# Two transformer blocks in one kernel: the convolution's weights on VectorE, a nested block inverse, more weight buffers and another order of transposes

## The chip, the cores and the metric

The kernel runs on one core of a Trainium2 chip, as one launch. Times are microseconds of device time, from the first to the last instruction of an execution and what the launch adds around it. Before the change the median of three runs is 3477.03 us (3469.45 to 3480.14). The engines are TensorE (PE in the trace; PEld is its weight load), VectorE (DVE), ScalarE (ACT), GpSimd (POOL) and SyncE (SP), which here issues nearly all DMAs. Each engine works through its own list of instructions in a fixed order and waits for the others at semaphores.

## The reference, cut to what matters

The model has 512 tokens of width 1024, a context of 256 tokens, and float32 throughout. Block 1 has two layers, block 2 two more:

```python
def first_block(x, c, ...):
    for i in range(2):
        shift, scale, gate = split(silu(c) @ mix_ada_w[i] + mix_ada_b[i], 3)
        h = x * (1 + scale) + shift
        y = _sgu_pool_mixer(h, ...) if i == 0 else _conformer_conv(h, ...)
        x = layer_norm(ALPHA * x + (1 + gate) * y)
        ...                                  # the same with ffn_ada_w and _conv_ffn
def _conformer_conv(h, w_in, dw, dw_b, ln_g, ln_b, w_out):
    a, g = split(h @ w_in, 2)                # 1024 channels each
    z = a * sigmoid(g)
    z = depthwise_conv(z, dw) + dw_b         # 31 taps a channel
    return silu(layer_norm(z)) @ w_out
def second_block(x, c, ctx, c_ctx, ...):
    for i in range(2):
        ml, mc = silu(c) @ w_ada[i] + b_ada[i], silu(c_ctx) @ w_ada[i] + b_ada[i]   # 6 chunks each
        u_lat, u_ctx = modulate(h_lat, ...), modulate(h_ctx, ...)   # rms_norm(h) * (1 + scale) + shift
        o = even_mixer(...) if i == 0 else odd_mixer(...)
        ...                                  # gated residuals and sqrelu_mlp, for context too in layer 0
def rwkv7_scan(f, d, s0, reverse):           # in even_mixer, forward and backward, 8 heads of 64
    def step(state, inp):
        sa = einsum(state, -kk_t)
        state = state * w_t + sa * (kk_t * a_t) + v_t * k_t
        return state, einsum(state, r_t)
```

## The kernel before, in words

**Matmuls.** Float32 matmuls are done as three matmuls of rounded parts: each operand is split in a high part (a rounding cast) and a low part (the difference), and `mm3` (L300) multiplies hi*hi, hi*lo and lo*hi. Weights come by `weights` (L280): SP loads a raw tile of 128x1024, for output weights the raw tile is multiplied by a gate (L287), ScalarE casts the high part (L289), and the low part is a difference (L290) on VectorE, or on the engine that `eng` names. The names in the trace end in the use: `wlo_cvin` is the low part of the convolution's input weights, `wraw_dn` a raw tile of output weights, `hTlo` the low part of transposed tokens.

**Order.** The code is written once through, and a scheduler puts the instructions of each engine in a list at build time; tile pools with a fixed number of buffers make an allocation wait for the last reader. Modulation (the products with `*_ada_w`) is cut into pieces that stand in the list `todo`; `fill` (L269) runs the next one wherever the code calls it, so that these matmuls (`adaps`, L209) lie between others. A piece of 512 columns has 4 weight loads of 512 KB on SP, 16 matmuls with 32 output rows each, a copy `adarows` on ScalarE and a store on SP. The first modulation (`ada_first`, L249) is done at the start, 4 pieces with whole 1 MB tiles from three buffers.

**The convolution** (`mixer1`, L584). For each of 8 channel blocks `gated` projects two times 128 channels (tile `cvps`, weights `cvin` with low parts on GpSimd) and multiplies by a sigmoid. Five blocks and 19 taps of a sixth are convolved on VectorE, one instruction a tap over 512 tokens (L621, L619; 169 of them in all); two blocks and 12 taps are convolved on TensorE with diagonal weights (`conv_pe`, tile `cvacc`): VectorE clears the borders, splits the block into `zh` and `zl` (L278 at the call L635) when `conv_pe` comes to it, one block later than its gate. Then the result is transposed (`cvt`), its statistics are taken on VectorE (L675), a square root follows by Newton steps, the result is normalised, transposed back and multiplied by `w_out`, whose first half of weights is prepared on GpSimd and whose second half on VectorE.

**The recurrence** (`recurrence`, L1346, with `operators`, L1447). The scan over 768 positions runs as six steps of 128 positions in two directions, each with 8 heads, so 12 blocks. A block needs the inverse of a unit lower triangular matrix of 64 per head and half. Its diagonal blocks of 16 are inverted on VectorE; GpSimd expands these to full tiles `X` and its transpose `XT`, and masks the matrix M for level 16 and level 32 (`MM`). Then per level: U = MM*XT (8 matmuls `pV`, copied by ScalarE), and `X` or `XT` gets X*U added (`pX`, addition L1483 on VectorE). Then `pW` multiplies by the operand `Aw`, and `pD` follows.

**The second block** starts by transposing its tokens and its context into `hT` (`hT2`, L861, with a parameter `first` that puts the context ahead), tile `hTps`, after their norms.

## Time and profile before

| what | us |
|---|---|
| median of three runs | 3477.03 |
| the profiled execution's own time | 3472.81 |
| its span, first to last instruction | 3471.0 |
| TensorE busy | 3216.5 (93%) |
| VectorE busy | 2053.2 (59%) |
| ScalarE busy | 1305.7 (38%) |
| GpSimd busy | 397.2 (11%) |

The trace is of one execution. Its stages, from the start of the span: first mixer to 192 us, feed-forward to 633, the convolution to about 914, feed-forward to 1338, the second block's first mixer with its projections to 1629, windowed attention to 1752, the recurrence to about 2110, feed-forward to 2727, the odd mixer to 3106, feed-forward to the end. A timeline row is: start, duration, engine, line, operation, output <- inputs, shape, how many instructions it stands for, and in brackets the idle time before it with what ended it. A group row ends with busy time, mean ns of one, and the idle time before the group by releaser. Line numbers are those of the kernel before.

### The profile page before, as it was taken

The numbers are of one execution on the slowest core, as the hardware profiler recorded it, in microseconds if no ns is written. First come the engines' busy times: TensorE is split into PE (matmuls) and PEld (weight loads), VectorE is DVE, ScalarE is ACT, GpSimd is POOL, SyncE is SP. The second block draws the span as 40 slices with busy tenths as digits, with TensorE's granted clock in tenths as the row PEclk, the third lists the DMA queues.
The fourth block names the chain that finished last, engine by engine and source line by source line (L and its number), as shares of the span: only waits on it lengthen the run. The fifth ranks groups of instructions, "written<-read, shape, count | busy, mean of one in ns | idle before, by whom it ended". The sixth has DMA issues, their size and how long they took to land. (4 is left out here: it accounts for less than half of the span.)

```text
span 3471.0 us, 50354 instructions
## 1 busy us (share of the span) xinstructions
PE 3216.5 (93%) x20031; PEld 2612.9 (75%) x20031; DVE 2053.2 (59%) x3772; ACT 1305.7 (38%) x2150; POOL 397.2 (11%) x218
## 2 busy tenths in 40 slices
PE   8989999868999998987898799999999998999998
PEld 5677777746776776875688798788888787878887
DVE  4675554897755567586767667533333735763445
ACT  3243332317423334443543334422222525753222
POOL 0020000540200000023033331010000200010001
PEclk9999999989999998998989899999999999999999
DMA  7645565440266432445322215672222365143332
GB/s 253 202 134 178 175 212 177 133 161 25 86 195 206 125 105 96 124 122 164 90 67 66 64 53 171 142 152 79 65 63 67 122 155 216 63 138 104 97 97 85
DMA packets 520693, 436.67 MB, mean 126 GB/s; under 512 B 91924, under 2 KB 450042, under 8 KB 518922
## 3 DMA queue, kind: packets, MB, share of 16 engines
q1 hardware_dynamic: 520458, 433.45, 41.4%
q8 instruction: 158, 2.59, 0.3%
q14 instruction: 77, 0.63, 0.1%
HBM read 368.96 MB, written 63.78 MB: 125 GB/s over the span
## 5 line engine op out<-in xcount | busy, mean ns | idle before, releaser
L302 PE MATMUL dnps<-whi_dn,hidh 128*128 128x512 f32 x1120 | 442.0, 395 | 3.5 <-ACT hidh L277 2.0
L303 PE MATMUL dnps<-wlo_dn,hidh 128*128 128x512 f32 x1120 | 438.9, 392 | 0.3
L304 PE MATMUL dnps<-whi_dn,hidl 128*128 128x512 f32 x1120 | 435.4, 391 | 1.2 <-DVE hidl L278 1.2
L290 DVE TENSOR_TENSOR wlo_dn<-wraw_dn,whi_dn 128x1024 fp32r<-128x1024 f32 x136 | 167.2, 1230 | 239.1 <-ACT whi_dn L289 238.3
L302 PE MATMUL upps<-hThi,whi_up 128*128 128x512 f32 (+1 forms) x768 | 295.7, 387 | 6.8 <-DVE hThi L277 6.7
L303 PE MATMUL upps<-hTlo,whi_up 128*128 128x512 f32 (+1 forms) x768 | 293.0, 383 | 4.8 <-DVE hTlo L278 4.8
L304 PE MATMUL upps<-hThi,wlo_up 128*128 128x512 f32 (+1 forms) x768 | 290.3, 379 | 0.0
L424 DVE TENSOR_TENSOR acc<-dnps,acc 128x512 f32<-128x512 f32 x200 | 136.7, 687 | 201.7 <-PE dnps L304 201.2
L302 PEld LDWEIGHTS dnps<-whi_dn,hidh 128*128 128x128 f32 x1120 | 210.2, 188 | 60.9 <-ACT hidh L277 7.0
L289 ACT CAST whi_dn<-wraw_dn 128x1024 fp32r<-128x1024 f32 x140 | 147.1, 1051 | 273.7 <-PE dnps L304 101.5
L303 PEld LDWEIGHTS dnps<-wlo_dn,hidh 128*128 128x128 f32 x1120 | 210.5, 188 | 47.1 <-issue 2.7
L304 PEld LDWEIGHTS dnps<-whi_dn,hidl 128*128 128x128 f32 x1120 | 209.8, 188 | 46.7 <-DVE hidl L278 3.4
L303 PE MATMUL up2ps<-hTlo,whi_ff 128*128 128x512 f32 (+1 forms) x576 | 214.5, 373 | 3.4 <-DVE hTlo L278 3.0
L302 PE MATMUL up2ps<-hThi,whi_ff 128*128 128x512 f32 (+1 forms) x576 | 212.7, 371 | 2.4 <-DVE hThi L277 2.4
L304 PE MATMUL up2ps<-hThi,wlo_ff 128*128 128x512 f32 (+1 forms) x576 | 212.1, 369 | 0.0
L290 DVE TENSOR_TENSOR wlo_up<-wraw_up,whi_up 128x1024 fp32r<-128x1024 f32 x88 | 111.1, 1262 | 135.5 <-ACT whi_up L289 134.6
L302 PEld LDWEIGHTS upps<-hThi,whi_up 128*128 128x128 f32 x768 | 147.2, 192 | 54.1 <-issue 12.4
L824 POOL TENSOR_TENSOR ag<-acc,gg 128x1024 f32<-128x1024 f32 x20 | 49.2, 2458 | 1124.8 <-DVE acc L424 1093.5
L303 PEld LDWEIGHTS upps<-hTlo,whi_up 128*128 128x128 f32 x768 | 147.5, 192 | 39.1 <-issue 9.9
L304 PEld LDWEIGHTS upps<-hThi,wlo_up 128*128 128x128 f32 x768 | 147.8, 193 | 26.1 <-issue 0.8
L289 ACT CAST whi_ff<-wraw_ff 128x1024 fp32r<-128x1024 f32 x64 | 67.2, 1052 | 245.9 <-PE dnps L304 202.3
L290 DVE TENSOR_TENSOR wlo_ff<-wraw_ff,whi_ff 128x1024 fp32r<-128x1024 f32 x64 | 80.8, 1264 | 126.7 <-ACT whi_ff L289 126.4
(528 smaller groups left out, 7431.0 us busy)
## 6 DMA issues: line engine op xcount, KB each, us to landing
adaw<-in_w_ada_dram SPq DMA_DIRECT2D x96, 512.0 KB
wraw_up<-in_ffn_w_up_dram SPq DMA_DIRECT2D x88, 512.0 KB
wraw_ff<-in_w_ff_dram SPq DMA_DIRECT2D x64, 512.0 KB
wraw_dn<-in_w_ff_dram SPq DMA_DIRECT2D x64, 512.0 KB
adaw<-in_ffn_ada_w_dram SPq DMA_DIRECT2D x48, 512.0 KB
wraw_dn<-in_ffn_w_down_dram SPq DMA_DIRECT2D x44, 512.0 KB
adaw<-in_mix_ada_w_dram SPq DMA_DIRECT2D x32, 512.0 KB
ab<-ab SPq DMA_DIRECT2D x32, 384.0 KB
```

The costliest lines, as they stand in the source:

```text
L289: nc.scalar.copy(hi, raw)
L290: (eng or nc.vector).tensor_tensor(lo, raw, hi, SUB)
L302: mm(out, a[0], b[0], start=first, stop=False)
L303: mm(out, a[0], b[1], start=False, stop=False)
L304: mm(out, a[1], b[0], start=False, stop=last)
L424: nc.vector.tensor_tensor(acc[:, t, c], p, acc[:, t, c], ADD)
L824: nc.gpsimd.tensor_tensor(ag, a, gg[:, 0 if t < NT else 1, :], MUL)
```

## The change

1. One mask `lo` (below the diagonal blocks of 16) takes the place of the masks for levels 16 and 32.
2. Modulation pieces have 256 columns where they had 512, so twice as many pieces and stores with half the size each; both raw tiles of a piece are loaded ahead of its matmuls. `fill` is called at more places: ahead of each weight in `ffn1`, in `mixer0` and in `gated`.
3. `ada_first` has 16 more tiles of 128x512 (four more 1 MB buffers), taken from the hidden tiles, so that all but the last of its loads have a buffer of their own.
4. In `mixer1` the low parts of the `cvin` weights and the gate products and low parts of the first half of `w_out` go from GpSimd to VectorE. `rounded` makes `zh`, `zl` and the rounded taps right behind the gate of a block that TensorE convolves; `conv_pe` gets them ready.
5. `operators`: the inverse by two levels becomes a nested form. NT is one product of MM and X (8 matmuls `pV`); then the operand is multiplied three times by NT, each time with the first operand added. Direction 0 multiplies by the diagonal inverse first (`pW`), direction 1 last, so direction 0 needs one expansion and direction 1 two.
6. `hT2` is called with `first=True`: the context is transposed ahead of the tokens.

Cut to its core (the list `todo` is cut anew to the same work in twice as many pieces, and the buffers of the recurrence are renamed):

```diff
+    c4.put("lo", np.concatenate([(t // 16 > u // 16) & (p[:, None] // 64 == q) for q in range(2)], 1))
...
     def ada_part(self, w, sil, c0, bufs=None):
 
-        nc = self.nc
-        acc = self.ps.tile([128, 512], F32, tag="tr", name="adaps", bufs=2)
+
+        nc = self.nc
         n = 512 if bufs else 256
-        for c in range(0, 512, n):
-            for h in range(0, KD, 4):
-                raw = bufs.pop(0) if bufs else self.adap.tile([128, 4, 256], F32, tag="adaw", name="adaw", bufs=self.nadaw)
-                nc.sync.dma_start(raw, w[128 * h:128 * h + 512, c0 + c:c0 + c + n].rearrange("(k p) c -> p k c", p=128))
+        acc = self.ps.tile([128, n], F32, tag="tr", name="adaps", bufs=2)
+        raw = []
+        for h in range(0, KD, 4):
+            b = bufs.pop(0) if bufs else self.adap.tile([128, 4, 256], F32, tag="adaw", name="adaw", bufs=self.nadaw)
+            if isinstance(b, list):
                 for k in range(4):
-                    nc.tensor.matmul(acc[32 * k:32 * k + 32, c:c + n], sil[:, h + k, :], raw[:, k, :], start=h == 0, stop=h > 0)
-        rows = self.wp.tile([128, 512], F32, tag="adar", name="adarows", bufs=1)
+                    nc.sync.dma_start(b[k], w[128 * (h + k):128 * (h + k) + 128, c0:c0 + n])
+            else:
+                nc.sync.dma_start(b, w[128 * h:128 * h + 512, c0:c0 + n].rearrange("(k p) c -> p k c", p=128))
+                b = [b[:, k] for k in range(4)]
+            raw.append(b)
+        for h, r in zip(range(0, KD, 4), raw):
+            for k in range(4):
+                nc.tensor.matmul(acc[32 * k:32 * k + 32], sil[:, h + k, :], r[k], start=h == 0, stop=h > 0)
+        rows = self.wp.tile([128, n], F32, tag="adar", name="adarows", bufs=1)
         nc.scalar.copy(rows, acc)
         return rows
 
     def ada_store(self, w, sil, c0, dst):
 
-        rows = self.ada_part(w, sil, c0)
-        for m in range(dst.shape[0]):
-            self.nc.sync.dma_start(dst[m, :, c0:c0 + 512], rows[m::32, :])
+        def piece(c):
+            rows = self.ada_part(w, sil, c)
+            for m in range(dst.shape[0]):
+                self.nc.sync.dma_start(dst[m, :, c:c + 256], rows[m::32, :])
+        return [partial(piece, c) for c in (c0, c0 + 256)]
...
-        bufs = [big[:, j] for j in range(3)]
+        hid = [b.bitcast(F32) for i in range(8) for b in self.hid(i)]
+        bufs = [big[:, j] for j in range(3)] + [hid[4 * j:4 * j + 4] for j in range(4)] + [big[:, 0]]
...
         def gated(f):
-            self.fill()
             pp = []
             for ff in (f, f + KD):
-                w = self.w_up(w_in, 128 * ff, "cvin", nc.gpsimd)
+                self.fill()
+                w = self.w_up(w_in, 128 * ff, "cvin")
...
-        def conv_pe(f):
+        def rounded(f):
...
+            return zh, zl, wh, wl
+
+        def conv_pe(f, zh, zl, wh, wl):
...
+        parts = []
         for j, f in enumerate(order):
             gated(f)
+            if f in taps_pe:
+                parts.append((f, *rounded(f)))
             for _ in range(14 if j else 0):
                 next(taps)
             if j >= 6:
-                conv_pe(order[j - 1])
+                conv_pe(*parts.pop(0))
                 for _ in range(12 if j == 6 else 24):
                     next(taps, None)
...
-            self.down(w_out, src[:4], acc, True, gate=gate, x=x, eng=nc.gpsimd)
+            self.down(w_out, src[:4], acc, True, gate=gate, x=x)
...
-            X, XT = (v8(bufs[x][d]) for x in ("X", "XT"))
-            for x, t in ((1, XT), (0, X)):
+            X, XT, Y = v8(bufs["X"]), v8(bufs["XT"][d]), v8(bufs["Y"][d])
+            for x, t in ((1, XT), (0, X))[:1 + d]:
...
-            for b in (16, 32):
-                U = v8(R.tile([128, 1024], F32, tag=f"tD{d}", name="U", bufs=2))
+            NT = v8(R.tile([128, 1024], F32, tag=f"tD{d}", name="NT", bufs=2))
+            for hs in H4:
+                nc.scalar.copy(NT[:, hs], mm4("pV", *((XT, MM) if d else (MM, XT)), hs))
+            if not d:
                 for hs in H4:
-                    nc.scalar.copy(U[:, hs], mm4("pV", MM[b], XT, hs))
-                for tr in ((1, 0) if b == 16 else (1 - d,)):
-                    for hs in H4:
-                        t = (XT if tr else X)[:, hs]
-                        vec.tensor_tensor(t, mm4("pX", *((X, U) if tr else (U, X)), hs), t, ADD)
-            XT = X if d == 1 else XT
-            for hs in H4:
-                nc.scalar.copy(Aw[:, hs], mm4("pW", XT, Aw, hs))
+                    nc.scalar.copy(Y[:, hs], mm4("pW", XT, Aw, hs))
+            first, at, to = (Aw, Aw, Y) if d else (Y, Y, Aw)
+            for _ in range(3):
+                for hs in H4:
+                    vec.tensor_tensor(to[:, hs], mm4("pX", NT, at, hs), first[:, hs], ADD)
+                at = to
+            if d:
+                for hs in H4:
+                    nc.scalar.copy(Aw[:, hs], mm4("pW", X, at, hs))
...
-                hT = self.hT2(n, mods)
+                hT = self.hT2(n, mods, first=True)
```

The lists of the engines show the change at these places. VectorE at the split for channel block 7 in the convolution, before: `hidl` with different numbers are the gated channel blocks, `hidh` their convolved results, L621 is a tap.

```order
L621 SCALAR_TENSOR_TENSOR hidh_5057<-hidl_5058,vec_e,hidh_5057 128x507
L621 SCALAR_TENSOR_TENSOR hidh_5055<-hidl_5056,vec_e,hidh_5055 128x506
L621 SCALAR_TENSOR_TENSOR hidh_5057<-hidl_5058,vec_e,hidh_5057 128x506
L621 SCALAR_TENSOR_TENSOR hidh_5055<-hidl_5056,vec_e,hidh_5055 128x505
L631 MEMSET zh 128x15
L632 MEMSET zh 128x15
L631 MEMSET zl 128x15
L632 MEMSET zl 128x15
L603 TENSOR_TENSOR hidl_5064<-cvps,sg 128x512
L278 TENSOR_TENSOR zl<-hidl_5066,zh 128x512
```

Now, at the same split (L285 is the split, L610 the gate product, L628 a tap):

```order
L639 MEMSET zh 128x15
L638 MEMSET zl 128x15
L639 MEMSET zl 128x15
L628 SCALAR_TENSOR_TENSOR hidh_5195<-hidl_5196,vec_e,hidh_5195 128x503
L610 TENSOR_TENSOR hidl_5204<-cvps,sg 128x512
L628 SCALAR_TENSOR_TENSOR hidh_5193<-hidl_5194,vec_e,hidh_5193 128x504
L628 SCALAR_TENSOR_TENSOR hidh_5195<-hidl_5196,vec_e,hidh_5195 128x504
L628 SCALAR_TENSOR_TENSOR hidh_5193<-hidl_5194,vec_e,hidh_5193 128x505
L285 TENSOR_TENSOR zl<-hidl_5204,zh 128x512
L628 SCALAR_TENSOR_TENSOR hidh_5195<-hidl_5196,vec_e,hidh_5195 128x505
L628 SCALAR_TENSOR_TENSOR hidh_5193<-hidl_5194,vec_e,hidh_5193 128x506
L628 SCALAR_TENSOR_TENSOR hidh_5195<-hidl_5196,vec_e,hidh_5195 128x506
```

The split `zl` of a block stood one block's taps behind that block's gate product; it now stands three taps behind it.

VectorE at the end of the convolution, where the statistics (`cvst`) are followed by the square root's steps (`newt`), before:

```order
L621 SCALAR_TENSOR_TENSOR hidh_5059<-hidl_5060,vec_e,hidh_5059 128x498
L675 BN_STATS cvst<-cvt 128x6
L621 SCALAR_TENSOR_TENSOR hidh_5059<-hidl_5060,vec_e,hidh_5059 128x497
L675 BN_STATS cvst<-cvt 128x6 x14
L687 BN_AGGR cvmv<-cvst 128x2 x4
L689 COPY cvvar<-cvmv 128x4
L353 TENSOR_SCALAR newt<-cvvar 128x4
L354 TENSOR_SCALAR newt<-newt 128x4
L361 TENSOR_TENSOR newt<-newt 128x4
L362 TENSOR_TENSOR newt<-newt 128x4
L363 SCALAR_TENSOR_TENSOR newt<-newt 128x4
```

And now:

```order
L688 BN_STATS cvst<-cvt 128x6 x2
L297 TENSOR_TENSOR wlo_dn<-wraw_dn,whi_dn 128x1024
L688 BN_STATS cvst<-cvt 128x6 x4
L700 BN_AGGR cvmv<-cvst 128x2 x4
L294 TENSOR_TENSOR wraw_dn<-wraw_dn,gate 128x1024
L702 COPY cvvar<-cvmv 128x4
L360 TENSOR_SCALAR newt<-cvvar 128x4
L361 TENSOR_SCALAR newt<-newt 128x4
L294 TENSOR_TENSOR wraw_dn<-wraw_dn,gate 128x1024
L368 TENSOR_TENSOR newt<-newt 128x4
L297 TENSOR_TENSOR wlo_dn<-wraw_dn,whi_dn 128x1024
L369 TENSOR_TENSOR newt<-newt 128x4
```

Output weights (L294, L297) that stood ahead of the last taps now lie behind the statistics and between the steps; the statistics themselves lie between the last taps.

TensorE in the recurrence, one block of direction 1, before:

```order
L323 MATMUL pD<-big 128x128 x16
L323 MATMUL pV<-big 128x128 x8
L323 MATMUL pX<-U,big 128x128 x8
L323 MATMUL pX<-big,U 128x128 x8
L323 MATMUL pV<-big 128x128 x8
L323 MATMUL pX<-big,U 128x128 x8
L323 MATMUL pW<-big 128x128 x8
L323 MATMUL pD<-big 128x128 x16
L323 MATMUL pz<-Z,big 64x64 x16
```

And now:

```order
L330 MATMUL pD<-big 128x128 x16
L330 MATMUL pV<-big 128x128 x8
L330 MATMUL pX<-big,NT 128x128 x24
L330 MATMUL pW<-big 128x128 x8
L330 MATMUL pD<-big 128x128 x16
L330 MATMUL pz<-Z,big 64x64 x16
L330 MATMUL PM<-AB 64x64 x15
```

One group of eight `pV` is gone, and the three rounds of `pX` stand in one run of 24, each round reading what the round before it left.

## Rows read from the trace of the kernel before

**Rows 1.** The page, part 1: busy time of each engine, its share, instructions.

```profile
PE 3216.5 (93%) x20031; PEld 2612.9 (75%) x20031; DVE 2053.2 (59%) x3772; ACT 1305.7 (38%) x2150; POOL 397.2 (11%) x218
```

**Rows 2.** Table by stage: us, busy PE PEld DVE ACT POOL, clock, DMA.

```profile
700.00:760.00 60.00, 49.66 (x279) 33.62 (x278) 60.00 (x64) 11.78 (x15) 34.53 (x10) 0.94 0.53 169
...
1752.00:2100.00 348.00, 309.76 (x3830) 288.01 (x3827) 243.20 (x515) 124.11 (x226) 124.05 (x80) 0.90 0.24 68
```

**Rows 3.** Timeline of PE, convolution: start, us, line, idle before and releaser.

```profile
745.21 1.08 PE L209 MATMUL adaps<-adaw,sil 128*32 128x256 f32 x8 [5.77 <-DMA adaw<-in_w_ada_dram]
...
776.83 0.76 PE L302 MATMUL cvacc<-zh,dg 128*128 128x512 f32 x1 [19.04 <-DVE zl L632]
...
802.90 0.47 PE L302 MATMUL cvacc<-zh,dg 128*128 128x512 f32 x1 [3.71 <-DVE zl L632]
```

**Rows 4.** Timeline of DVE, convolution.

```profile
735.35 24.65 DVE L621 SCALAR_TENSOR_TENSOR hidh<-hidl,vec_e,hidh 128x498 f32<-128x498 f32 x19
...
760.53 16.11 DVE L621 SCALAR_TENSOR_TENSOR hidh<-hidl,vec_e,hidh 128x509 f32<-128x509 f32 x18
...
777.24 0.68 DVE L278 TENSOR_TENSOR zl<-hidl,zh 128x512 fp32r<-128x512 f32 x1
...
813.61 21.80 DVE L621 SCALAR_TENSOR_TENSOR hidh<-hidl,vec_e,hidh 128x497 f32<-128x497 f32 x28
848.77 0.43 DVE L675 BATCH_NORM_STATS2 cvst<-cvt 128x6 f32<-128x256 f32 x1 [13.36 <-PE cvt L667]
```

**Rows 5.** Groups of POOL, 633 to 855 us: busy, mean ns, idle before.

```profile
L290 POOL TENSOR_TENSOR wlo_cvin<-wraw_cvin,whi_cvin 128x1024 fp32r<-128x1024 f32 x15 | 39.7, 2654 | 40.0 <-ACT whi_cvin L289 36.9 <-PE adaps L209 3.1
L287 POOL TENSOR_TENSOR wraw_dn<-wraw_dn,gate 128x1024 f32<-128x1024 f32 x4 | 16.8, 4207 | 17.5 <-DMA wraw_dn<-in_cv_w_out_dram 8.4 <-PE adaps L209 5.1 <-issue 4.0
L290 POOL TENSOR_TENSOR wlo_dn<-wraw_dn,whi_dn 128x1024 fp32r<-128x1024 f32 x4 | 10.8, 2696 | 25.9 <-ACT whi_dn L289 25.9
```

**Rows 6.** Groups of DVE, 633 to 855 us: busy, mean ns, idle.

```profile
L621 DVE SCALAR_TENSOR_TENSOR hidh<-hidl,vec_e,hidh 128x503 f32<-128x503 f32 (+15 forms) x169 | 147.2, 916 | 1.9
L278 DVE TENSOR_TENSOR hTlo<-hTf,hThi 128x256 fp32r<-128x256 f32 x16 | 14.8, 939 | 0.2
```

**Rows 7.** Groups of DVE, 813 to 836 us, GpSimd idle.

```profile
L621 DVE SCALAR_TENSOR_TENSOR hidh<-hidl,vec_e,hidh 128x499 f32<-128x499 f32 (+15 forms) x29 | 21.6, 745 | 1.0
```

**Rows 8.** Groups of DVE, first feed-forward stage, 192 to 633 us.

```profile
L290 DVE TENSOR_TENSOR wlo_up<-wraw_up,whi_up 128x1024 fp32r<-128x1024 f32 x41 | 50.2, 1224 | 67.8 <-ACT whi_up L289 67.4
...
L278 DVE TENSOR_TENSOR hTlo<-hTf,hThi 128x256 fp32r<-128x256 f32 x16 | 10.6, 680 | 0.1
```

**Rows 9.** Waits of SP, 640 to 800 us: total, times, longest.

```profile
SPq L285 <- POOL wlo_dn L290: 29.1, 4, 8.5
SPq L218 <- ACT adarows L211: 9.3, 6, 2.1
```

**Rows 10.** Timeline of PE in one block of the recurrence.

```profile
1870.32 1.95 PE L323 MATMUL pV<-big 128*128 128x128 f32 x16
1872.11 2.00 PE L323 MATMUL pX<-big,U 128*128 128x128 f32 x16
1873.99 2.05 PE L323 MATMUL pW<-big 128*128 128x128 f32 x16
```

**Rows 11.** Groups of POOL in the recurrence, 1752 to 2100 us.

```profile
L1460 POOL TENSOR_TENSOR big<-Xd,consts 128x1024 f32<-128x1024 f32 x12 | 29.2, 2437 | 22.4 <-PE pV L323 15.9 <-PE pW L323 6.4
```

**Rows 12.** Groups of PE in the recurrence: the state products.

```profile
L323 PE MATMUL P<-AB 64*64 64x64 f32 x1152 | 48.5, 235 | 18.4 <-DVE big L1422 15.0 <-DVE WhThi L1422 2.9 <-ACT M L1383 0.2
```

**Rows 13.** Timeline of DVE in the same block of the recurrence.

```profile
1873.24 0.69 DVE L1483 TENSOR_TENSOR big<-pX,big 128x512 f32<-128x512 f32 x1 [2.04 <-PE pX L323]
```

**Rows 14.** Timeline of PE at the second block's start.

```profile
1345.99 0.69 PE L337 MATMUL hTps<-consts,acc 128*128 128x128 f32 x2 [7.75 <-ACT acc L814]
```

**Rows 15.** Table of windows at the start, columns as in rows 2.

```profile
25.00:30.00 5.00, 5.00 (x18) 3.95 (x17) 4.14 (x12) 2.87 (x6) 0.00 (x0) 0.56 1.05 409
```

**Rows 16.** Timeline of PE at the start.

```profile
30.34 1.07 PE L209 MATMUL adaps<-adaw,silc 128*32 128x512 f32 x8
```

More of the change, by code (lines that the diff above doesn't have):

```diff
@@ L521, in mixer0 @@
         for h in range(4):
-            if h == 2:
-                self.fill()
+            self.fill()
             w = self.w_up(w_in, 128 * h, "inu")
@@ L543, in mixer0 @@
         for g, win in enumerate(WINDOWS):
+            self.fill()
             w = self.w_up(w_in, 1024 + 128 * g, "inz")
@@ L752, in ada @@
             i, part = phases[k]
-            return [lambda q=q: self.ada_store(ap[f"{part}_ada_w"][i], sil, 512 * q, ada1[k]) for q in qs]
-        ada2 = [lambda j=j: self.ada_store(ap["w_ada_2"][j // 12], sil2, 512 * (j % 12), self.ada_d[j // 12])
-                for j in range(24)]
+            return [f for q in qs for f in self.ada_store(ap[f"{part}_ada_w"][i], sil, 512 * q, ada1[k])]
+        ada2 = [f for j in range(24) for f in self.ada_store(ap["w_ada_2"][j // 12], sil2, 512 * (j % 12), self.ada_d[j // 12])]
         def columns():
```

27 lines of the change are left out of this document (10 added, 17 removed).

## Prediction

> **What bounds the kernel now.** I read the page's busy shares, then the table by stage, then the timelines of the stages with idle on TensorE. TensorE is busy 3216.5 of 3471.0 us [rows 1]: over the whole span it is the bound, and only its idle time, or matmuls that go, can be won. Two of the stages that the change touches have much of that idle. One is the second mixer of the first block (the convolution, 633 to 860 us). In its middle VectorE is busy 60.00 of 60 us and TensorE 49.66 [rows 2], and TensorE stops 5.77, 19.04 and 3.71 us in single waits [rows 3]. The other is the recurrence (1752 to 2100), where TensorE is busy 309.76 of 348 us [rows 2]: there the matmuls themselves are the bound.
>
> Why VectorE is the bound of the convolution is seen in its taps. With GpSimd beside it, 19 of them take 24.65 us, 1.30 each; later, with GpSimd idle, 28 take 21.80, 0.78 each [rows 4]. The long wait of 19.04 ends with `zl`, a split of one channel block, which VectorE issues at 777.24 behind a run of 18 taps that began at 760.53: its order is fixed, so TensorE waits for taps that it does not need. After the last tap (813.61 + 21.80 = 835.4) VectorE itself is idle 13.36 us, until TensorE, late by those waits, has transposed the result [rows 4].
>
> **The change part by part.** All sums are made against the profiled run, 3472.8 us; it lies 4.2 us under the median of the three runs.
>
> *Convolution: work moved from GpSimd to VectorE.* GpSimd loses 15 differences of 2.65 us, 4 products with the gate of 4.21 and 4 differences of 2.70: 39.7 + 16.8 + 10.8 = 67.3 us [rows 5]. What that beside it cost VectorE: 169 taps at 0.916 against 0.745 when alone, 28.9 us; 16 differences `hTlo` at 0.939 against 0.680 in the feed-forward stage, 4.1 [rows 6, 7, 8]. Together 33.0 us go. What VectorE gains in work: 15 + 8 operations of 128x1024 at 1.224 [rows 8] are 28.2 us. So its load falls by only 4.8 us; most of the win must come from order. Three gate products and one difference for the second half of w_out (4.9 us), that stood ahead of the last taps, now come behind the statistics. The last tap then ends at 835.4 - 4.8 - 4.9 = 825.7. On TensorE the split for the three blocks that it convolves is made right behind the gate, with 3 taps ahead of it where 18 stood, so the waits of 19.04 and 3.71 go, and so does the 5.77: that one was a modulation load that sat on SP behind a buffer which GpSimd held (29.1 us in four such waits [rows 9]). The transposes that ended the 13.36 us of idle move by these 28.5 us, from 848.8 to 820.3. The later of the two, 825.7, is 23.1 us before 848.8. Three of the operations that moved back lie in the short chain behind the statistics, 3.7 us: 19.4 remain. The new differences sit in VectorE's order, though, where they wait for ScalarE's rounding with taps queued behind them, and TensorE waits for them in turn; on the other side, smaller operations than the taps are freed too, and I take **-19**. Bounds: -5 if only the load of VectorE falls, -29 if all three of TensorE's waits go and nothing else ends last.
>
> A rule in the Trainium skill, SBUF — State Buffer, "Who interferes with whom", bears on the size of this: a VectorE instruction with two operands from SBUF contends with a GpSimd instruction that reads SBUF, and the loser is blocked for the whole of it. The trace agrees in kind (1.30 against 0.78 us a tap), but a full block would cost VectorE nearer the 67.3 us of GpSimd's work than the 33.0 counted here; that is the second rival.
>
> *Recurrence: nested inverse.* Each of 12 blocks (six steps, two directions) has 8 `pV` matmuls where it had 16; each is two records, so 192 of them go. Sixteen records stand 1.79 us apart from the next group without idle (1870.32 to 1872.11) [rows 10], 0.112 each: 21.5 us off TensorE. `pX`, `pW` and `pD` keep their numbers, and so do VectorE's additions. Two of four copies per block leave ScalarE, and 6 expansions and 10 masks leave GpSimd, 16 x 2.4 = 38 us [rows 11]; the state products wait 15.0 us for VectorE in this stage [rows 12], of which I count 4 as won. Against it: the three `pX` rounds now depend on each other. A round of 16 records takes TensorE 1.88 us (1872.11 to 1873.99); its second half may start 0.06 us after the addition of the half before it (1873.24 + 0.69 to 1873.99) [rows 10, 13]. One half's loop is 0.69 addition + 0.06 + 0.94 half a round + 0.20 before the addition = 1.89: as long as the round itself. I take 0.15 us of loss each, 36 rounds, +5. **-20** in all. Bounds: -8 if the rounds lose 0.5 each and no wait is won, -28 if none is lost and half of the 15.0 is won.
>
> *Context first in the second block.* Its mixer begins with TensorE idle 7.75 us, waiting for the first tokens' norm [rows 14]. The context's transposes need no norm of that moment, and now stand ahead of the tokens' in TensorE's order. TensorE had to do that work anyway, so at most the wait is won: **-4**, between 0 and -8.
>
> *Start: four more buffers.* They let SP issue the second half of the first weights without waiting. But the transfers before 25 us fill the DMA engines already (share 1.05 at 409 GB/s), they come in the same order, and from 25 on TensorE is busy 5.00 of 5 us [rows 15]: nothing is won. The `adaps` matmuls there ran as four at once in 1.07 us [rows 16]; in the new order groups of 4, 2, 1, 1, 2, 1, 1, 4 stand where four fours stood, most of a microsecond for each of the 4 new groups: **+3**, from 0 to +5.
>
> *Smaller modulation pieces.* The bytes are the same; issues on SP grow by 81 rows. In the convolution SP waited 9.3 us in six waits for `adarows` [rows 9], with weight loads behind; twice as many such stores may double that, but the loads run ahead. Cost 0, at most +9. The context's own items come late in the second feed-forward either way, and I price them at nothing.
>
> Sum: -19 - 20 - 4 + 3 = -40, so 3472.8 - 40 = **3433** (rounded, and not moved by the 4.2 us to the median, which are less than the runs differ among themselves).
>
> **The rivals.** (a) *The convolution wins only its load.* Sixteen differences in VectorE's order each wait for ScalarE, with taps behind; TensorE loses on the first tiles what it wins on the last. For it: VectorE has no idle between 700 and 760. Against it: the taps behind are short. The term is -5 where it was -19 and the context wins nothing: 3472.8 - 5 - 20 + 3 = 3451. (b) *GpSimd cost VectorE all its time.* Then VectorE's last tap ends at 835.4 - 67.3 + 28.2 - 4.9 = 791 and TensorE is the bound of the convolution at 820, -29; in the recurrence the 38 us of GpSimd bring back the waits of 15.0 rather than 4 of them, -31 there: 3472.8 - 29 - 31 - 4 + 3 = 3412. (c) *Slower: the serial rounds.* Each addition of a round queues on VectorE behind work of the other direction or the next step (the products and expansions share that engine), and TensorE, with nothing else in its order, stops. Without the rounds' term the sum is -45, so it decides from 45/36 = 1.25 us per round; at 2.1 us, three additions of 0.69 ahead of it, +30: 3503. Against it: before, each block also had five dependent steps on TensorE ahead of `pD`, and waits for these additions hardly show. (d) *Neither does much*: the rounds lose 0.5 each and the convolution ends on the added differences: about 3470.
>
> **How the numbers follow.** My forecast has 0.54 (3418 to 3442 by its own), (a) 0.18, (b) 0.14, (d) 0.08, (c) 0.06. A measurement here tells 0.3%, about 10 us, from no change. Faster: forecast, (a) and (b), and little of (d): 0.87. Same: (d) 0.08. Slower: 0.05. The range 3406 to 3461 takes in (b) at its low end and (a) at its high end.
>
> **What would show it.** Convolution: no GpSimd beside taps, taps near 0.75 us throughout; the wait for `zl` gone; the first statistics about 25 us sooner, and if they are not, TensorE waiting for `wlo_cvin` shows (a). Recurrence: `pV` halved, the stage 20 us shorter; TensorE idle before `pX`, released by the additions, shows (c). Second block: the 7.75 us filled. Start: first `vps` at the same time. The prediction is wrong if the convolution is not shorter, or if the rounds stand apart on TensorE.

## The result, and the profile after

The changed kernel takes 3430.89 us (median of four runs, 3430.77 to 3433.27) where the kernel before takes 3474.97 on the same chip: a ratio of 0.9875, with a 95% interval of 0.9858 to 0.9892. The forecast was 3433, a fall of 40 us; the medians fell by 44.1 and the two profiled executions by 42.0. Its profiled execution took 3430.79 us, with a span of 3428.8, against 3472.8 and 3471.0 before. The busy times, which answer to [rows 1], are these (engine, busy us, share of the span, instructions):

```profile
PE 3184.9 (93%) x19839; PEld 2583.5 (75%) x19839; DVE 2031.7 (59%) x3794; ACT 1290.3 (38%) x2170; POOL 294.6 (9%) x178
```

TensorE has 192 instructions and 31.6 us of work less, GpSimd 102.6 us less. VectorE has 22 instructions more and yet is busy 21.5 us less: that row says that its instructions got shorter.

Where the 42.2 us of span went, stage by stage, read from the first and last instructions of each stage in the two traces:

| Stage | before, us | after, us | difference | predicted |
|---|---|---|---|---|
| start, to the last product of the first projection (`vps`) | 59.3 | 62.8 | +3.5 | +3 |
| from there to the first feed-forward (`upps`) | 132.9 | 136.3 | +3.4 | 0 |
| first transposes of the convolution to its last product (`cvb`) | 239.3 | 213.5 | -25.8 | -19 |
| feed-forward behind it, its first products | 397.3 | 393.5 | -3.8 | 0 |
| from the end of that feed-forward to the first matmul of the windowed attention (`sc`) | 290.7 | 295.6 | +4.9 | -4 |
| windowed attention, first `sc` to the first state product | 124.4 | 121.2 | -3.2 | 0 |
| recurrence, first state product to last `pz` | 352.5 | 332.0 | -20.5 | -20 |

The rest is -0.7. Not all of these are effects: the windowed attention, with the same list of TensorE's instructions in all 14 traces of this study, took 117.6 to 127.9 us. TensorE was busy 92 us there in the shortest, at a mean granted clock of 0.94 of 2.4 GHz, and 103 us in the longest, at 0.84. The stretch ahead of the first feed-forward scatters in the same way: with TensorE's and VectorE's lists of the changed kernel it took 131.6, 134.1, 136.3 and 139.2 us in four traces, at mean granted clocks of 1.00, 0.98, 0.96 and 0.95. So neither the -3.2 nor the +3.4 is shown to be an effect.

**Convolution.** The table by stage has the stretch of [rows 2] again (start:end, us, busy PE PEld DVE ACT POOL, granted clock, DMA share, GB/s), and the groups of VectorE in the stage answer to [rows 6] (busy, mean ns, idle before):

```profile
700.00:760.00 60.00, 58.92 (x327) 41.53 (x326) 55.06 (x88) 16.96 (x35) 0.00 (x0) 1.00 0.63 196
```

```profile
L628 DVE SCALAR_TENSOR_TENSOR hidh<-hidl,vec_e,hidh 128x500 f32<-128x500 f32 (+15 forms) x169 | 117.2, 737 | 1.4
L297 DVE TENSOR_TENSOR wlo_cvin<-wraw_cvin,whi_cvin 128x1024 fp32r<-128x1024 f32 x15 | 19.8, 1330 | 4.0 <-ACT whi_cvin L296 3.9
L285 DVE TENSOR_TENSOR hTlo<-hTf,hThi 128x256 fp32r<-128x256 f32 x16 | 10.6, 681 | 0.1
```

In the middle TensorE is busy 58.92 of 60 us where it was 49.66, and VectorE 55.06 where it was 60.00: the bound has changed engine. The mean tap takes 737 ns where it took 916, as it did before when GpSimd was idle (745, [rows 7]); `hTlo` takes 681 where it took 939, again the time it has elsewhere (680, [rows 8]). The new differences wait only 3.9 us for ScalarE's rounding. Over the whole stage TensorE's idle time falls from 51.5 to 27.9 us, and its busy time, for as many records, only from 187.9 to 185.6 (mean granted clock 0.89 and 0.91). Its waits of 5.77, 19.04 and 3.71 us [rows 3] are gone; what is left of its waits (engine, tile, line, what it waits for: total, times, longest) comes mostly from the chain at the stage's end:

```profile
PE cvb L716 <- ACT acc L710: 8.9, 1, 8.9
PE cvt L680 <- ACT acc L690: 7.8, 3, 5.3
PE cvps L309 <- DVE hThi L284: 4.1, 3, 1.9
PE cvps L310 <- DVE hTlo L285: 2.8, 2, 2.0
PE adaps L215 <- DMA adaw<-in_w_ada_dram: 1.7, 5, 0.4
```

The mean of 916 ns hides what happened to the taps. The next two lines give the shortest, median and longest tap in ns (after x169:), before and in the changed kernel:

```profile
L621 DVE SCALAR_TENSOR_TENSOR hidh<-hidl,vec_e,hidh x169: 718/736/2909, 670.9 to 850.1; 128x509 f32<-128x509 f32 x12, 128x510 f32<-128x510 f32 x12, 128x511 f32<-128x511 f32 x12, 128x497 f32<-128x497 f32 x11
L628 DVE SCALAR_TENSOR_TENSOR hidh<-hidl,vec_e,hidh x169: 712/739/752, 673.5 to 826.8; 128x509 f32<-128x509 f32 x12, 128x510 f32<-128x510 f32 x12, 128x511 f32<-128x511 f32 x12, 128x497 f32<-128x497 f32 x11
```

Before, 154 of the 169 taps took at most 754 ns, as they do now. The other 15 took 2.26 to 2.91 us, and each of them began while GpSimd was at one of its operations and ended 0.53 to 0.55 us after it. One pair of the kernel before:

```profile
672.76 2.63 POOL L290 TENSOR_TENSOR wlo_cvin<-wraw_cvin,whi_cvin 128x1024 fp32r<-128x1024 f32 x1 [3.65 <-ACT whi_cvin L289]
673.17 2.76 DVE L621 SCALAR_TENSOR_TENSOR hidh<-hidl,vec_e,hidh 128x500 f32<-128x500 f32 x1
```

So GpSimd did not slow all taps a little: each of its operations beside them held up one VectorE instruction until it was done.

**Recurrence.** The whole stage (columns as above) and, for one block, TensorE's and VectorE's timelines (start, us, line, what; in brackets the idle before and what ended it), which answer to [rows 2, 10, 13]:

```profile
1730.00:2063.00 333.00, 292.97 (x3698) 267.36 (x3697) 240.73 (x517) 111.98 (x204) 86.87 (x64) 0.91 0.26 74
...
1840.06 2.05 PE L330 MATMUL pV<-big 128*128 128x128 f32 x16
1841.94 5.88 PE L330 MATMUL pX<-big,NT 128*128 128x128 f32 x48
1847.81 2.02 PE L330 MATMUL pW<-big 128*128 128x128 f32 x16
...
1843.09 0.69 DVE L1498 TENSOR_TENSOR big<-pX,big 128x512 f32<-128x512 f32 x1 [2.23 <-PE pX L330]
...
1845.03 0.69 DVE L1498 TENSOR_TENSOR big<-pX,big 128x512 f32<-128x512 f32 x1 [0.36 <-PE pX L330]
...
1846.97 0.69 DVE L1498 TENSOR_TENSOR big<-pX,big 128x512 f32<-128x512 f32 x1 [0.36 <-PE pX L330]
```

The three rounds run as one row of 48 records: 1841.94 to 1847.81, 5.87 us, 0.122 a record against 0.112 before. The additions of one half stand 1.94 us apart (1843.09, 1845.03, 1846.97), where the loop was worked out at 1.89. TensorE's waits here, which answer to [rows 12]:

```profile
PE P L330 <- DVE big L1434: 14.9, 5, 5.2
PE pX L330 <- DVE big L1498: 8.0, 8, 3.9
```

The state products wait 14.9 us for VectorE where they waited 15.0: nothing of that was won, though GpSimd lost work in the stage. The rounds wait 8.0 us. That is no loss, though: before, TensorE waited about as long for the additions of the two levels, at `pW`:

```profile
PE pW L323 <- DVE big L1483: 5.4, 1, 5.4
PE pW L323 <- DVE WhThi L1483: 3.1, 3, 1.6
```

**Second block's start.** TensorE's, ScalarE's and VectorE's timelines, which answer to [rows 14]:

```profile
1296.33 0.60 PE L344 MATMUL hTps<-consts,acc 128*128 128x128 f32 x4
...
1341.18 1.15 PE L344 MATMUL hTps<-consts,acc 128*128 128x128 f32 x4 [27.31 <-ACT hTf L346]
...
1294.69 1.01 ACT L346 ACTIVATE hTf<-hTps,mod,G 128x256 f32<-128x256 f32 x2
...
1338.87 1.15 ACT L826 ACTIVATE acc<-x,mv 128x1024 f32<-128x1024 f32 x1 [2.14 <-DVE mv L366]
1340.57 1.02 ACT L346 ACTIVATE hTf<-hTps,mod,G 128x256 f32<-128x256 f32 x2
...
1338.56 0.21 DVE L366 TENSOR_SCALAR mv<-newt 128x1 f32<-128x1 f32 x1
1338.69 0.48 DVE L284 CAST hTchi<-hTf 128x256 fp32r<-128x256 f32 x2
```

The wait of 7.75 us is not filled but has become 27.31. The first context transposes do run early, by 1296.33. ScalarE moves them out into `hTf`, which has three buffers; those come free when VectorE has split them (the cast `hTchi`, then a difference), and the first such cast stands in VectorE's list behind the norm of the last tokens (`mv`, 1338.56). The next `hTf` comes at 1340.57. It also stands behind that norm's `acc` in ScalarE's own list (1338.87); whether a fourth buffer would have let it run earlier was not tried. The tokens' transposes, some of whose norms are long done, stand behind the context's on TensorE. Why the casts come so late in VectorE's list was not settled. The work after the wait runs denser than before, so the stage loses 4.9 us and not 19.6 (27.31 - 7.75).

**Start.** TensorE's timeline, which answers to [rows 16]:

```profile
28.95 0.62 PE L215 MATMUL adaps<-hidh,silc 128*32 128x512 f32 x1
...
32.49 1.04 PE L215 MATMUL adaps<-hidh,silc 128*32 128x512 f32 x2
...
34.35 1.04 PE L215 MATMUL adaps<-hidl,silc 128*32 128x512 f32 x2
```

The first row is one record of a group of four that still starts together; the other two stand alone. One narrow matmul by itself (two records) takes 1.04 us, as much as four that start together took before (eight records, 1.07).

### The profile page after: what moved, and what is told of

The parts are those of the page before. It is cut to its first block, busy times and chain, and to the rows that moved or that the text cites. A ratio compares the mean times of both kernels' runs of the same rounds, so it can differ in the third digit from the quotient of the medians.

```text
span 3428.8 us, 50127 instructions
## 1 busy us (share of the span) xinstructions
PE 3184.9 (93%) x19839; PEld 2583.5 (75%) x19839; DVE 2031.7 (59%) x3794; ACT 1290.3 (38%) x2170; POOL 294.6 (9%) x178
## 3 DMA queue, kind: packets, MB, share of 16 engines
q1 hardware_dynamic: 521194, 433.39, 42.2%
## 5 line engine op out<-in xcount | busy, mean ns | idle before, releaser
L297 DVE TENSOR_TENSOR wlo_dn<-wraw_dn,whi_dn 128x1024 fp32r<-128x1024 f32 x140 | 172.2, 1230 | 276.0 <-ACT whi_dn L296 275.0
L309 PEld LDWEIGHTS dnps<-whi_dn,hidh 128*128 128x128 f32 x1120 | 210.6, 188 | 59.3 <-ACT hidh L284 10.4
L297 DVE TENSOR_TENSOR wlo_up<-wraw_up,whi_up 128x1024 fp32r<-128x1024 f32 x88 | 111.0, 1262 | 156.6 <-ACT whi_up L296 152.0
L296 ACT CAST whi_up<-wraw_up 128x1024 fp32r<-128x1024 f32 x88 | 92.2, 1049 | 177.0 <-PE upps L310 60.3
L297 DVE TENSOR_TENSOR wlo_ff<-wraw_ff,whi_ff 128x1024 fp32r<-128x1024 f32 x64 | 81.1, 1268 | 130.2 <-ACT whi_ff L296 129.9
```

The source lines that it names most:

```text
L296: nc.scalar.copy(hi, raw)
L297: (eng or nc.vector).tensor_tensor(lo, raw, hi, SUB)
L309: mm(out, a[0], b[0], start=first, stop=False)
```

## The experiments

Each is given with its time, its ratio to the kernel before and the interval, and the stage that it bears on. They ran on several chips, each beside the kernel before, whose median there was 3474.4 to 3477.9 us, so ratios compare better than times (0.001 is 3.5 us). A stage is read from one execution, which can lie 15 us from its kernel's median.

**What won in the convolution.** The change has two parts there: work moved from GpSimd to VectorE, and the split of TensorE's three blocks made earlier. They were built into the kernel before, together and one by one.

```diff
+        def rounded(f):            # the split, made right behind the gate
-        def conv_pe(f):
+        def conv_pe(f, zh, zl, wh, wl):
+            if f in taps_pe: parts.append((f, *rounded(f)))
# and, the other part:
-                w = self.w_up(w_in, 128 * ff, "cvin", nc.gpsimd)
+                w = self.w_up(w_in, 128 * ff, "cvin")
-            self.down(w_out, src[:4], acc, True, gate=gate, x=x, eng=nc.gpsimd)
+            self.down(w_out, src[:4], acc, True, gate=gate, x=x)
```

Both:

> The kernel before with the convolution's part of the change alone: low parts and gate products on VectorE, and the split right behind the gate. In the changed kernel's trace the stage from the first transposes to the last ones behind the convolution takes 213.5 us where it took 239.3. Theory (the parts add up): 25 us less, 3450 us. Rival (part of the 25.8 us comes from the smaller modulation pieces that lie in that stage): 15 us less, 3460.

Measured: 3451.11 us, 0.9921 [0.9891, 0.9952]; the stage took 210.9 us (239.3 before).

Only the early split:

> The kernel before with only the split right behind the gate; GpSimd keeps its work. Theory (load and order both count, as in the prediction): TensorE's waits of 19.04 and 3.71 us go, but VectorE's taps stay slow and end near 835 us, the statistics can start only there: 14 us less, 3461. Rival 'order alone': 22 us or more less, 3453. Rival 'load alone': within 4 us of before.

Measured: 3470.2, 0.998 [0.997, 0.9991], 6 us below the kernel before by the medians; the stage 237.7, -1.6. Its VectorE group of taps and TensorE's waits in the stage:

```profile
L621 DVE SCALAR_TENSOR_TENSOR hidh<-hidl,vec_e,hidh 128x503 f32<-128x503 f32 (+15 forms) x169 | 149.3, 927 | 1.9
```

```profile
PE cvacc L302 <- ACT dg L646: 12.5, 2, 11.2
PE adaps L209 <- DMA adaw<-in_w_ada_dram: 7.8, 3, 6.5
```

The waits for `zl` are gone, and TensorE waits 12.5 us for ScalarE's `dg` and 7.8 for a transfer in their place. The long wait for `dg` is one for VectorE again: ScalarE, which makes `dg`, sat idle until VectorE had reached the next block's gate product, behind 102 taps:

```profile
778.05 0.68 DVE L603 TENSOR_TENSOR hidl<-cvps,sg 128x512 f32<-128x512 f32 x1
778.76 0.62 ACT L277 CAST zh<-hidl 128x512 fp32r<-128x512 f32 x1 [13.83 <-DVE zh L631]
```

So the moved split only handed the wait on. The mean tap is as long as ever.

Only the change of engine, with the split left late:

> The kernel before with only the move of low parts and gate products from GpSimd to VectorE; the split stays one block late. Theory (both count): the taps fall to 0.74 us, but TensorE still waits some 16 us for the split, and is later than VectorE at the end: 9 us less, 3466. Rival 'order alone': 5 us less or none. Rival 'load alone': 20 us or more less, 3455.

Measured: 3449.54, 0.9916 [0.9898, 0.9933]; the stage 209.7, -29.6. The same views:

```profile
L621 DVE SCALAR_TENSOR_TENSOR hidh<-hidl,vec_e,hidh 128x508 f32<-128x508 f32 (+15 forms) x169 | 117.0, 738 | 1.4
...
L277 DVE CAST hThi<-hTf 128x256 fp32r<-128x256 f32 x16 | 7.2, 465 | 1.2 <-ACT hTf L339 1.2
...
L619 DVE TENSOR_SCALAR hidh<-hidl,vec_e 128x512 f32<-128x512 f32 x5 | 2.7, 540 | 0.0
```

and, in the kernel before, the two smaller groups that [rows 6] do not show:

```profile
L277 DVE CAST hThi<-hTf 128x256 fp32r<-128x256 f32 x16 | 9.7, 612 | 1.9 <-ACT hTf L339 1.9
L619 DVE TENSOR_SCALAR hidh<-hidl,vec_e 128x512 f32<-128x512 f32 x5 | 6.9, 1371 | 0.0
```

TensorE's waits with the engine changed alone:

```profile
PE cvb L703 <- ACT acc L697: 8.3, 1, 8.3
PE cvt L667 <- ACT acc L677: 3.7, 2, 2.5
PE cvps L303 <- DVE hTlo L278: 3.6, 2, 1.9
```

The wait for `zl`, 22.8 us in the stage before, is down to 0.3, although the code of the split was not touched. The build laid VectorE's list anew, however: the first split stands behind 90 taps where it stood behind 103, and runs at 748.85 where it ran at 777.24. At the mean of 0.92 us, 13 taps are 12 us, an estimate, so part of the 28 us is place and the larger part is shorter work ahead of it. TensorE's waits for modulation weights fall too, from 8.3 to 0.6 us; how much of the gain is loads that no longer stand behind GpSimd's buffers was not told apart. Both one-part expectations missed, in opposite directions. Of the rivals, "load alone" holds for the change of engine (20 us or more); for the early split it gave within 4 us of before, and 6 were measured. The long wait of 19.04 us had been read as a fault of the order alone; most of it was VectorE's list being late.

**Is it GpSimd?** To the changed kernel, 128 subtractions of 128x128 on GpSimd are added beside the convolution; their results are read by nothing. TensorE's and VectorE's instructions stay as they are.

```diff
+                for k in range(KD):
+                    side = self.small.tile([128, 128], F32, tag="side", name="side", bufs=1)
+                    nc.gpsimd.tensor_tensor(side, w[0][:, k], self.c["ident"], SUB)
```

> The changed kernel, and GpSimd besides subtracts a constant from each high part of the convolution's 16 weight tiles, eight pieces of 128x128 a tile, into a tile that nobody reads; VectorE and TensorE have the same lists as in the changed kernel. Theory (GpSimd's work beside VectorE's costs VectorE about 0.63 us for each us of it, 42.7 for 67.3 in the kernel before): some 40 us of GpSimd work, 25 us more on VectorE, of which its 14.7 us of idle time in the stage take a part: 12 to 25 us more, 3450; taps from 0.74 toward 0.9 us. Rival (the convolution gained because nothing waits for GpSimd's results and buffers any more): within 4 us, 3431, taps at 0.74.

Measured: 3453.99, 0.9925 [0.9908, 0.9942], 23 us above the changed kernel by the medians and 17 by the ratios; the stage 230.0 (213.5). Groups of GpSimd and VectorE in the stage:

```profile
L607 POOL TENSOR_TENSOR side<-whi_cvin,consts 128x128 f32<-128x128 f32 x120 | 91.5, 763 | 23.8 <-ACT whi_cvin L296 15.2
L631 DVE SCALAR_TENSOR_TENSOR hidh<-hidl,vec_e,hidh 128x500 f32<-128x500 f32 (+15 forms) x169 | 129.1, 806 | 1.4
L297 DVE TENSOR_TENSOR wlo_cvin<-wraw_cvin,whi_cvin 128x1024 fp32r<-128x1024 f32 x15 | 22.1, 1481 | 11.0 <-ACT whi_cvin L296 11.0
```

The mean tap goes from 737 to 806 ns by nothing but work on another engine, and the stage is 16.5 us longer, with VectorE's idle time as before (15.0 for 14.7): GpSimd's presence is a cause, not a companion. Its operations are short here, and so are the stops: 54 taps took 0.85 us or more, none over 1.03 (shortest, median and longest tap after x169:).

```profile
L631 DVE SCALAR_TENSOR_TENSOR hidh<-hidl,vec_e,hidh x169: 718/744/1025, 692.2 to 853.1; 128x509 f32<-128x509 f32 x12, 128x510 f32<-128x510 f32 x12, 128x511 f32<-128x511 f32 x12, 128x497 f32<-128x497 f32 x11
```

The size was missed: the added work came to 91.5 us on GpSimd, where some 40 had been expected, and cost VectorE 16.4 us of busy time.

**Nested inverse alone** in the kernel before:

```diff
-                        vec.tensor_tensor(t, mm4("pX", *((X, U) if tr else (U, X)), hs), t, ADD)
+                nc.scalar.copy(NT[:, hs], mm4("pV", *((XT, MM) if d else (MM, XT)), hs))
...
+            for _ in range(3):
+                for hs in H4:
+                    vec.tensor_tensor(to[:, hs], mm4("pX", NT, at, hs), first[:, hs], ADD)
+                at = to
```

> The kernel before with only the nested inverse in the recurrence. Theory: 192 records of 0.112 us go from TensorE, the rounds lose little: 20 us less, 3455, the stretch from the first state product to the last of pz 332 us where it was 352.5. Rival (part of the 20 us comes from elsewhere, the rounds lose 0.5 us each): 8 us less, 3467.

Measured: 3461.27, 0.9957 [0.9943, 0.997], -15 us by the runs; in its profiled execution, the fastest of the seven by 13 us, the stage took 329.9 us (352.5 before). The gain is there alone. Its size shows best in the traces of all experiments: the eight with the nested inverse took 329.9 to 337.2 us in the stage, the six without it 352.5 to 356.1.

**Tokens first again** in the changed kernel:

```diff
-                hT = self.hT2(n, mods, first=True)
+                hT = self.hT2(n, mods)
```

> The changed kernel with the tokens turned ahead of the context again. In the changed kernel's trace TensorE stops 27.31 us at the second block's start where it stopped 7.75 us before, and the stretch from the end of the feed-forward to the windowed attention's first matmul is 295.6 us where it was 290.7. Theory (the context ahead costs: the tokens' transposes queue on TensorE behind the context's, and these wait for buffers that ScalarE and VectorE free only behind the last tokens' norms): the wait falls back to 8 us, the stretch by 5 us, 3426. Rival (as predicted, the context first gains up to 4 us, and the 4.9 us come from elsewhere): 3435.

Measured: 3431.32, 0.9869 [0.985, 0.9888]. In the trace the wait is back to 7.70 us and the stage to 291.1 (295.6): the stage answers as expected, and the ratio is 2 us under the changed kernel's 0.9875, well inside the intervals. TensorE's group of these transposes from 1290 to 1385 us (busy, mean ns, idle before and by what), in the changed kernel and then with the tokens first:

```profile
L344 PE MATMUL hTps<-consts,acc 128*128 128x128 f32 x48 | 11.0, 339 | 28.2 <-ACT hTf L346 28.1
```

```profile
L344 PE MATMUL hTps<-consts,acc 128*128 128x128 f32 x48 | 13.3, 377 | 12.5 <-ACT acc L826 9.9 <-ACT hTf L346 2.6
```

**The context between the tokens**, behind the first pair of token tiles and ahead of the last:

```diff
-        parts = [lambda: self.to_hT(hT, n[:, 0:NT, :], NT, 0, *mods[0])]
+        parts = [lambda a=a: self.to_hT(hT, n[:, a:a + 2, :], 2, 128 * a, *mods[0]) for a in range(0, NT, 2)]
-            parts.insert(0 if first else 1, ...)
+            parts.insert(1 if first else 2, ...)
```

> The changed kernel with the context's transposes between those of the first and of the last two token tiles. Theory (buffers and norms set the wait): the first tokens' transposes start when their norm is there, about 8 us of wait, and the context fills waits for the last two tiles' norms, which with tokens first took 2 to 3 us more: 3424. Rival (any place ahead of the last tokens costs, since the context's splits wait on VectorE behind the norms): 3431.

Measured: 3426.6, 0.9857 [0.9839, 0.9875]; the stage 289.7, 5.9 below the changed kernel:

```profile
L344 PE MATMUL hTps<-consts,acc 128*128 128x128 f32 x48 | 13.1, 381 | 10.4 <-ACT acc L826 7.7 <-ACT hTf L346 2.6
```

The wait is 7.73 us, as before the change; what the tokens wait for is the norm again.

**Three 1 MB buffers again** at the start:

```diff
-        bufs = [big[:, j] for j in range(3)] + [hid[4 * j:4 * j + 4] for j in range(4)] + [big[:, 0]]
+        bufs = [big[:, j % 3] for j in range(8)]
```

> The changed kernel with three 1 MB buffers for the first modulation weights, as before, in place of seven. The changed kernel's last product of the first projection ends at 62.8 us, before at 59.3. Theory (the single narrow matmuls of the four new buffers lose what four at once had): the 3.5 us come back, 3427.5. Rival (the later order at the start comes from the smaller pieces): no difference, 3431. Third (the buffers help): 3434.

Measured: 3430.35, 0.9863 [0.9846, 0.988]. TensorE's timeline has the four together again:

```profile
29.72 1.06 PE L215 MATMUL adaps<-adaw,silc 128*32 128x512 f32 x8
```

The last `vps` ends at 58.7 us (62.8): the start is as it was, so the four buffers had won nothing there. The median moves by half a microsecond, the ratio by 4 us, inside the intervals.

**The smaller modulation pieces.** First undone in the changed kernel (512 columns, and the places of the fills as before), then put alone into the kernel before, then there together with both convolution parts:

```diff
# the pieces, as the change has them
+        return [partial(piece, c) for c in (c0, c0 + 256)]
# undone
-            return [f for q in qs for f in self.ada_store(ap[f"{part}_ada_w"][i], sil, 512 * q, ada1[k])]
+            return [lambda q=q: self.ada_store(ap[f"{part}_ada_w"][i], sil, 512 * q, ada1[k]) for q in qs]
```

> The changed kernel with modulation pieces of 512 columns and the fills at the places of before; all else as changed. Theory (the smaller pieces lose about 3 us in the first mixer, where TensorE now waits 1.1 to 2.2 us for adaw loads five times, and 2.6 us in the convolution, 213.5 us against 210.9 with the convolution's part alone): 5 us less, 3426. Rival (they win in the feed-forward stages, 3.8 us in the second): 3432.

> The kernel before with only the modulation pieces of 256 columns and the fills at more places. Theory (undoing them in the changed kernel cost 13 us by the medians, some 8 by the stages, most in the second feed-forward): 8 to 13 us less, 3466. Rival (as predicted, nothing or a loss): 3475 to 3484.

> The kernel before with the convolution's part of the change and the modulation pieces of 256 columns, and nothing else (no nested inverse, three buffers, tokens first). Alone the convolution's part gave 25 us and the pieces nothing, but without the pieces the changed kernel is 13 us slower. Theory (the pieces pay only once VectorE and GpSimd no longer set the convolution's pace): 13 us less than the convolution's part alone, 3438. Rival (they add as measured alone): 3451. Third (the 13 us come with the inverse or from the scatter of the recurrence and windowed stages): 3445 to 3451, with the first block's stages within 2 us of those of the convolution's part alone.

Measured: undone, 3444.09, 0.9907 [0.9889, 0.9924], 13 us slower than the changed kernel by the medians and 11 by the ratios, whose intervals just overlap, where a gain had been expected; alone, 3478.62, 1.0003 [0.9988, 1.0018], nothing, as the prediction had priced them; with the convolution parts 3446.68, 0.9918 [0.99, 0.9935], against 0.9921 for those parts alone, and no first-block stage differs by 2 us between the two. So the pieces are worth nothing alone, and why undoing them costs 11 to 13 us stays open.

One stage does answer to them, the first products of the second feed-forward. The six traces with the pieces and fills of before took 394.8 to 400.0 us in it, the eight with the smaller pieces 391.5 to 395.4, 4 us less in the mean. This gain is there with the pieces alone (392.3), so the other stages must give it back; ahead of the first feed-forward and in it they cost a microsecond or two, no more than these stages scatter. Of the execution with the pieces undone, which took 21 us longer than the changed kernel's, some 8 us are in the first block, 6.5 of them in this stage; most of the rest lies in the windowed attention (127.9 us, at the lowest granted clock of all, 0.84) and the recurrence, which scatter by that much with the same lists.

With the pieces alone the wait for `zl` is there as ever, which fits the rest:

```profile
PE cvacc L310 <- DVE zl L640: 25.9, 2, 22.2
```

**The two losses undone together**, three buffers and the context between the tokens, in the changed kernel:

> The changed kernel with three buffers for the first modulation weights, and the context's transposes between the first and the last two token tiles. Theory (both terms add: 3.6 us at the start, 5.9 at the second block's start): 9 us less than the changed kernel, 3422. Rival (a term hides behind other work): 3427.

Measured: 3421.77 (3417.46 to 3427.27), 0.9836 [0.982, 0.9852], 9.1 us under the changed kernel by the medians and 14 by the ratios, whose intervals do not overlap, and the lowest median of all. The last `vps` ends at 58.0, and the second block's start takes 286.9 us (295.6); the transposes there, from 1300 to 1385:

```profile
L343 PE MATMUL hTps<-consts,acc 128*128 128x128 f32 x48 | 12.4, 365 | 10.5 <-ACT acc L825 7.7 <-ACT hTf L345 2.7
```

## Why the prediction was right, and where its steps failed

The time was right, 3433 for 3431, and the sum is mostly made of the right terms. But one reason in it was wrong, and two terms with the wrong sign or price met an underestimate.

*Convolution, -19 forecast, -25.8 in the trace.* The step that failed is "So its load falls by only 4.8 us; most of the win must come from order". From the stage's first transpose to the end of its statistics VectorE was busy 199.0 us and idle 24.6 before, 180.1 and 14.7 after (a stretch in which two operations overlap counted once). Compared over that stretch, before with the kernel that only changes the engine: taps 31.6 us less, `hTlo` 4.5, `hThi` 2.4 and the five products that begin the taps of a block (L619) 4.2, together 42.7 freed where 33.0 were counted. The taps were sized nearly right (28.9 counted), by a mean that no single tap had; what was left out are the smaller operations beside them. Added were 22.6 (28.2 counted, of which 4.9 behind the statistics: 23.3). So 20 us net where the prediction's own numbers give 9.7. The rest of the failure is in attribution: TensorE's waits were given to the order and VectorE's load only to the taps' end. The early split alone wins 1.6 us of stage, and the change of engine alone wins all of it, 29.6, the build's new order of VectorE's list included. In the early split the wait moves on to the next instruction of VectorE's list that TensorE needs. A wait that ends with an instruction standing behind 18 taps can be cured by moving it or by shortening the work ahead of it; the trace before shows the wait but not which cure leaves no other wait behind it. A small misreading beside it: the taps did not end at 835.4, since two more stood between the statistics (849.12 and 850.10).

*The second rival*, that GpSimd costs VectorE all its time, came in between: 42.7 us for GpSimd's 67.3, 0.63 of each. In the experiment with small subtractions it was 16.4 for 91.5, 0.18. Neither is a rate at which VectorE runs slower. Beside the taps ran 17 of GpSimd's operations, and each held up one VectorE instruction by 2.0 us in the mean, 15 taps and two of the five products of L619. These read one array; the two took 2.6 us and the other three 0.54, hence the mean of 1371 ns. What GpSimd's time did not cost is the part in which a VectorE instruction was already running, and its own delays: one of its products lasted 8.52 us, and for most of these the taps went on at their usual length.

The Trainium skill, SBUF — State Buffer, "Who interferes with whom", has a VectorE instruction with two SBUF inputs contend with a GpSimd instruction that reads SBUF, and whichever comes second stopped until the first is done. The trace agrees, instruction by instruction (a tap of 2.76 us beside GpSimd's 2.63, where 0.74 is usual). The prediction set such a full stop against its own 33.0 us and expected nearer 67.3 from it; the stop was full, and it cost 42.7.

*Recurrence, -20 forecast, -20.5 measured* (and TensorE's busy time in the stage 21.8 less, 314.8 to 293.0; 21.5 were counted for the 192 matmuls). The two small terms were both wrong and cancelled, which was luck. The +5 us for rounds that now depend on each other did not come: TensorE waits 8.0 us for their additions, 0.22 a round, but before it waited 8.5 for the additions at `pW`. The 4 us counted as won from the state products' waits of 15.0 did not come either (14.9), though GpSimd is busy 37 us less in the stage (38 counted). So the third rival, serial rounds that stop TensorE, is refuted: even without what it saved it would be 0.22 us a round, where it decided from 1.25.

*Second block, -4 forecast, +4.9 measured.* The step "TensorE had to do that work anyway, so at most the wait is won" failed, and so did its bounds, 0 and -8: it looked at what the moved instructions wait for, not at what carries their results away. Moved ahead, they held three buffers behind a cast that comes late, and all later transposes stood behind them. Both other orders undo it (291.1 and 289.7), so the order is the cause; that it acts through the buffers is read from one timeline.

*Start, +3 forecast, +3.5 measured*, by the mechanism named, groups of one for groups of four; undoing it gives 4 us back. A further 3.4 us before the first feed-forward were not forecast; identical lists scatter by more there. *Smaller pieces, 0 forecast*: alone 0, but by cancellation, with 4 us won in the second feed-forward and given back elsewhere; in company open. The -3.8 of that stage comes with the pieces and not with the context's new place, since it is there without it.

The terms that were off nearly cancel: -7 (convolution) and -4 (feed-forward) against +9 (second block's start) and +3.4 (after the start, perhaps scatter), with -3 of scatter in the windowed attention. So the closeness of 3433 to 3431 is in part luck.

## What to carry to other kernels

Work on GpSimd beside a busy VectorE is not free: subtract what it adds to VectorE's instructions, the smaller ones too, before calling it moved off. Look at the longest instructions of a group and not at its mean: a few that were stopped look like many that are slow. When one engine waits for an instruction that stands late in another's list, ask both whether it can stand earlier and whether the list can be shorter, and test each alone. Instructions that are placed earlier must have somewhere to put their results: follow them to the instruction that frees their buffers.

## What the runs showed that was not expected

What GpSimd's work costs VectorE is a sum of single stops and no share of its time: 42.7 us for 23 operations of 128x1024, 1.9 each, and 16.4 us for some 120 of 128x128, 0.14 each (spans on GpSimd are rough in these profiles). On GpSimd itself a 128x128 subtraction beside VectorE's taps took 763 ns, where a 128x1024 difference, of eight times the elements, took 2654 [rows 5]; whether that is a fixed cost or the contention from its other side was not told apart.

Single executions of identical instruction lists differ by several microseconds a stage. The first convolution experiment and the one with 512-column pieces have the same TensorE list in the convolution, and took 210.9 and 215.3 us in it, with 1.2 and 3.8 us of waits for modulation weights and mean granted clocks of 0.93 and 0.91. Differences of 4 us, as for the start and the context's place, show in their stage of the trace but lie inside the intervals of four runs, about 6 us either way; the two together, 13.5 in their stages, are clear of them.
